# GpSimd's products given a choice of VectorE, and a scheduler that counts their shared port, in a hybrid LRU, GLA and SSD mixer

## The chip, the core and the metric

The kernel runs on one core of one Trainium2 chip. The metric is the device time in microseconds from launch to end on that core; shorter is better. The core's engines run side by side and wait for each other by semaphores. In the rows below PE is TensorE (PEld its weight loads), DVE is VectorE, ACT is ScalarE, POOL is GpSimd, SP the queue that issues the DMAs. Each engine works through its own queue strictly in the order in which the program lists it, so an instruction that waits holds up all that stand behind it.

## The reference, cut to what matters

Two layers (DEPTH = 2) work on 512 latent tokens and 256 context tokens of width 1024, all in float32. Layer 1 computes no output for the context tokens.

```python
s = h @ w_in                                    # one input projection feeds three branches
ya = bidir(lru_scan,    gates(conv(s[0])))      # h_t = a_t h_{t-1} + sqrt(1 - a_t^2) (i_t x_t)
yb = bidir(gla_chunked, q, k, v, logg)          # gated linear attention
yc = bidir(ssd_chunked, x*dt, dt*A, B, C)       # Mamba-2 state-space duality, in chunks
    # per chunk: m = cb * exp(cum_t - cum_s);  y = m x + (C state) exp(cum)
    #            state = state * exp(cum_end) + B^T (x * decay)
pa = (ya * silu(s[1])) @ w_pa
pb = (rmsnorm(yb) * silu(s[5])) @ w_pb
pc = rmsnorm((yc + d*x) * silu(s[7])) @ w_pc
out = x + gate * rmsnorm((g0*pa + g1*pb + g2*pc) @ w_out)
```

## The kernel before

**Tiling.** Every activation lies with 128 channels on the partitions and the tokens (768 in layer 0, the last 512 of them in layer 1) along the free axis. Each weight tile of 1024 columns comes by DMA (`raw`), is split into a high part (`wh`, a cast, by ACT or DVE) and the rest (`wl = raw - wh`, a subtraction on DVE), and the projections are three matmuls each (high by high, high by low, low by high) into the PSUM tiles `pp`. `ahead` counts the halves split in advance. Other matmuls and transposes write the PSUM tiles `aux`.

**Stages.** A layer runs through the SSD branch (32 heads in four groups `g`, each in two half groups `hg` of four heads), then GLA, then LRU, then the output projections. While a branch's small operations run, PE does the projections of the next items, `pc` and the gates, whose order is a fixed list.

**The SSD stage.** For each half group three streams run side by side. `ssd_states` goes over the chunks in both directions: `ssd_update` forms `xw` (the inputs scaled by their decay), the next state `sb` or `sf` as the old one scaled by `etr`, the split of `xw` into `xwh` (cast) and `xwl` (subtraction), three matmuls, and the sum into the new state. `ssd_ms` forms the 128x512 matrix `rr`: a DMA brings it, ACT adds a bias per head, DVE merges the two directions (`pred`, a COPY_PREDICATED), ACT takes the exponential, and then it is multiplied by `cb`. `ssd_scan` forms `y`, tokens on the partitions: `xt` times `kd`, plus matmul results, each scaled by `tokp` into `yi` and added. `y` is then transposed and multiplied into `gz`. `ssd_finish` adds four squares (`r`) and norms.

**The LRU stage.** `lru_rec` forms, for each of eight blocks and two directions, `w` as the square of `av` (128x768), and then `w`, `th`, `hf` and `hb` on DVE by products and scans.

**What goes where.** Helpers record one operation each: `tt` (product or sum of two tensors), `sub`, `copy`, `stt`, `ts`, `act`, `mm`. In `tt`, the argument `pool=True` sends the operation to POOL without a choice. So it stands with `xw`, the state products `sb` and `sf`, the product `rr` by `cb`, `y` from `xt` and `kd`, the sums of squares `r` and the square of `av`. `sub` with `pool=True`, `copy` and `affine` already let the scheduler choose between two engines.

**The scheduler.** The order in every queue is made when the program is built. Each stream is a generator that yields its next operation. `Sched.loop` takes, again and again, the operation that could start first by a model of the engines (`start_of`: when the engine is free and the data there, plus 200 ns for a hop between engines and a slack for the engine), with priorities for ties. Where an operation has several ways, it takes the one whose modelled start plus cost is least. The costs are straight lines:

```python
    def gcost(self, n):
        return 2.4 * n + 100
...
    def vcost(self, n, x, fast=False):
        return (0.52 if fast and x.space != PSUM else 1.04) * n + 69
```

No stretch of one engine by another is in this model.

## Time and profile before

| | us |
|---|---|
| median of 3 runs | 2781.73 (2781.67 to 2783.38) |
| the profiled execution | 2780.03 |
| its span, from the first instruction to the last | 2778.3 |
| mean granted clock of PE | 0.992 |

The profiled execution is longer than its span by 1.7 us, which lie around the instructions. Its rows tell, by engine and stage, how long instructions ran, and in which order. An instruction's row begins when it is taken up and ends when it is done. The next one of the same engine may be taken up before that, so the distance from one start to the next is what an instruction costs a full queue, and its duration is what an instruction that waits for it sees. The ends of matmuls are modelled, so PE's idle time shows best as that of its weight loads, PEld. By the source lines, the stages stand in the span so: the SSD stage of layer 0 from about 105 to 690, its LRU stage from about 1150 to 1400, the SSD stage of layer 1 from about 1640 to 2110, its LRU stage from about 2500 to 2660.

### The profile page before, as it was taken

To read this page: it belongs to the slowest core of one execution; us is meant where nothing else is said; L and a number is where in the kernel's file an instruction comes from. 1 tells how busy PE (TensorE), PEld (TensorE's weight loads), DVE (VectorE), ACT (ScalarE), POOL (GpSimd) and SP (SyncE) were. 2 spreads that over 40 slices of the span, in tenths; PEclk is the share of its full clock that TensorE was granted. 3 is DMA by queue.
4 is the path that set the end of the run, shared out by engine and by line. 5 is a ranking of instruction groups with operands and counts; after the bars stand their busy time and mean duration, and the time that the engine had idled before them with its cause. 6 is when DMAs were issued, how large, how long until landed. Compare 5 with 4: busy or idle time off the path is not lost.

```text
span 2778.3 us, 42828 instructions
## 1 busy us (share of the span) xinstructions
PE 2701.1 (97%) x16166; PEld 2344.8 (84%) x16166; DVE 2099.5 (76%) x3920; ACT 1186.7 (43%) x2274; POOL 584.2 (21%) x684
## 2 busy tenths in 40 slices
PE   7999999999999999999999999999999999999998
PEld 5888888888888888888889878788888888888877
DVE  5688988888555554668956879989897866568987
ACT  5355545454413331226622554545453333245732
POOL 1143525334000000001100224445251000001100
PEclk9999999999999999999999999999999999999999
DMA  6242323333352223552256434333334532243255
GB/s 212 73 126 69 113 68 102 79 96 93 102 182 73 73 61 94 158 162 57 76 169 209 140 89 109 84 91 105 86 107 114 167 84 76 81 147 103 54 158 195
DMA packets 448255, 307.99 MB, mean 111 GB/s; under 512 B 17189, under 2 KB 423281, under 8 KB 448049
## 3 DMA queue, kind: packets, MB, share of 16 engines
q1 hardware_dynamic: 448048, 305.26, 38.1%
q8 instruction: 127, 2.08, 0.3%
q14 instruction: 80, 0.65, 0.1%
HBM read 273.15 MB, written 32.06 MB: 110 GB/s over the span
## 4 chain that ended last, share of the span: by engine, by line
PE 74%; DVE 18%; issue 3%; DMA 2%; ACT 2%; POOL 1%; SPq 0%; DVEq 0%; POOLq 0%; ACTq 0%
PE pp L394 61%; PE aux L394 10%; DVE wl L343 2%; PE aux L398 2%; DVE r L364 2%; DVE xa L364 1%; DVE wh L329 1%; DMA ada<-in_ada_w_dram 1%; DVE xwl L343 1%; DVE rr L388 1%; DMA rr<-cumd 1%; PE aux L530 1%; DVE y L360 1%; DVE hf L360 0%; DVE xwh L329 0%
## 5 line engine op out<-in xcount | busy, mean ns | idle before, releaser
L394 PE MATMUL pp<-hl,wh 128*128 128x256 f32 (+2 forms) x2624 | 768.8, 354 | 0.2 <-DVE hl L343 0.2
L394 PE MATMUL pp<-hh,wh 128*128 128x256 f32 (+2 forms) x2624 | 761.5, 353 | 7.6 <-DVE xa L364 5.6
L394 PE MATMUL pp<-hh,wl 128*128 128x256 f32 (+2 forms) x2624 | 761.6, 352 | 0.6 <-DVE wl L343 0.6
L394 PEld LDWEIGHTS pp<-hh,wh 128*128 128x128 f32 (+1 forms) x2624 | 487.2, 189 | 68.6 <-ACT av L319 3.9
L394 PEld LDWEIGHTS pp<-hl,wh 128*128 128x128 f32 (+1 forms) x2624 | 489.0, 189 | 62.1 <-issue 2.6
L394 PEld LDWEIGHTS pp<-hh,wl 128*128 128x128 f32 (+1 forms) x2624 | 488.2, 189 | 61.1 <-DVE wl L343 1.0
L343 DVE TENSOR_TENSOR wl<-raw,wh 128x512 fp32r<-128x512 f32 (+1 forms) x628 | 467.8, 748 | 44.6 <-ACT wh L328 15.3
L329 DVE CAST wh<-raw 128x512 fp32r<-128x512 f32 (+1 forms) x401 | 191.7, 478 | 369.1 <-PE pp L394 362.8
L319 ACT ACTIVATE rr<-rr,tokp 128x128 f32<-128x128 f32 x640 | 202.5, 390 | 108.6 <-DMA rr<-cumd 108.2
L328 ACT CAST wh<-raw 128x512 fp32r<-128x512 f32 (+1 forms) x227 | 138.7, 617 | 241.3 <-PE pp L394 203.5
L319 ACT ACTIVATE r<-pp 128x768 f32<-128x768 f32 (+1 forms) x112 | 78.6, 702 | 253.1 <-PE pp L394 250.9
L360 POOL TENSOR_TENSOR xw<-xt,tokp 128x256 f32<-128x256 f32 x160 | 121.8, 761 | 270.0 <-ACT xt L328 188.6
L712 POOL TENSOR_SCALAR ss<-ss 128x1 f32<-128x1 f32 x52 | 14.2, 272 | 698.1 <-ACT ob L319 665.6
L360 POOL TENSOR_TENSOR w<-av 128x768 f32<-128x768 f32 x32 | 53.3, 1665 | 422.3 <-ACT av L319 355.5
L360 POOL TENSOR_TENSOR rr<-rr,cb 128x512 f32<-128x512 f32 x80 | 110.7, 1383 | 123.1 <-ACT rr L319 118.2
L394 PE MATMUL pp<-oh,wh 128*128 128x512 f32 (+1 forms) x384 | 121.1, 365 | 0.0
L394 PE MATMUL pp<-ol,wh 128*128 128x512 f32 (+1 forms) x384 | 120.8, 365 | 0.0
L394 PE MATMUL pp<-oh,wl 128*128 128x512 f32 (+1 forms) x384 | 119.4, 361 | 0.0
L394 PE MATMUL pp<-yh,wh 128*128 128x512 f32 (+1 forms) x384 | 116.9, 358 | 1.3 <-DVE r L364 1.3
L394 PE MATMUL pp<-yh,wl 128*128 128x512 f32 (+1 forms) x384 | 116.9, 358 | 0.0
L394 PE MATMUL pp<-yl,wh 128*128 128x512 f32 (+1 forms) x384 | 115.7, 355 | 0.0
L394 PE MATMUL pp<-wh,hl 128*128 128x256 f32 x384 | 108.9, 284 | 0.0
(270 smaller groups left out, 5343.4 us busy)
## 6 DMA issues: line engine op xcount, KB each, us to landing
raw<-in_w_in_dram SPq DMA_DIRECT2D x208, 512.0 KB
rr<-cumd SPq DMA_DIRECT2D x160, 256.0 KB
raw<-in_w_out_dram SPq DMA_DIRECT2D x40, 512.0 KB
raw<-in_w_pc_dram SPq DMA_DIRECT2D x32, 512.0 KB
raw<-in_ada_w_dram SPq DMA_DIRECT2D x32, 512.0 KB
ada<-in_ada_w_dram SPq DMA_DIRECT2D x8, 1024.0 KB
raw<-in_w_pb_dram SPq DMA_DIRECT2D x16, 512.0 KB
raw<-in_w_pa_dram SPq DMA_DIRECT2D x16, 512.0 KB
```

The costliest lines, as they stand in the source:

```text
L319: self.nc.scalar.activation(out, in_, func, **kw)
L328: yield from self.any_op([("ACT", self.acost(n, in_), lambda: self.nc.scalar.copy(out, in_)), ("DVE", self.vcost(n, in_, True), lambda: se ...
L329: ("DVE", self.vcost(n, in_, True), lambda: self.nc.vector.tensor_copy(out, in_))],
L343: ways = [("DVE", self.vcost(n, a), lambda: self.nc.vector.tensor_tensor(out, a, b, ALU.subtract))]
L360: yield from self.op("POOL" if pool else "DVE", [out], [a, b], cost, lambda: eng.tensor_tensor(out, a, b, op))
L364: lambda: self.nc.vector.scalar_tensor_tensor(out, a, s, b, op0, op1))
L388: lambda: self.nc.vector.copy_predicated(out, mask, data))
L394: lambda: self.nc.tensor.matmul(out, lhsT, rhs, start=start, stop=stop))
L398: yield from self.op("PE", [out], [in_, idn], 108, lambda: self.nc.tensor.transpose(out, in_, idn))
L530: yield from self.op("PE", [ps], [self.scf, w], w.free_size() / 2.4, lambda: self.nc.tensor.matmul(out, lt, w, start=k < 4, stop=k >= 4, t ...
L712: yield from self.op("POOL", [r], [ss], 150, lambda: self.nc.gpsimd.tensor_scalar(r, ss, 1.0 / width, EPS, ALU.mult, ALU.add))
```

## The change

Four things are edited. `tt` with `pool=True` now has two ways, DVE first and POOL second, and the scheduler takes the one with the earlier modelled end. The scheduler keeps, for DVE and for POOL, the last six modelled spans in which it used the port that both share: every POOL operation, and every DVE operation marked with `port` whose tensors are all outside PSUM. `shared` lengthens an operation's modelled cost by the time in which it overlaps such spans of the other engine, both where a choice is made and where the operation is entered. The marks are set in `any_op` (by default), `stt`, `ts` and `vcopy`. Nothing that is computed changes.

```diff
--- before.py
+++ after.py
@@ -151,6 +151,7 @@
         self.cells = {}
         self.eng_free = {"PE": 0.0, "DVE": 0.0, "ACT": 0.0, "POOL": 0.0, "SP": 0.0}
         self.dma_free = 0.0
+        self.port = {"DVE": [], "POOL": []}
         self.warm_up = HAM_WINDOW
         self.act_set = None
         self.seq = 0
@@ -184,14 +185,21 @@
                 r = c.r + slack
         return r
 
-    def op(self, eng, outs, ins, cost, emit):
-        yield from self.any_op([(eng, cost, emit)], outs, ins)
-
-    def any_op(self, ways, outs, ins):
-
+    def op(self, eng, outs, ins, cost, emit, port=False):
+        yield from self.any_op([(eng, cost, emit)], outs, ins, port)
+
+    def shared(self, eng, start, cost):
+
+        for a, b in self.port["POOL" if eng == "DVE" else "DVE"]:
+            cost += max(0.0, min(b, start + cost) - max(a, start))
+        return cost
+
+    def any_op(self, ways, outs, ins, port=True):
+
+        port = port and all(x.space != PSUM for x in outs + ins if x is not None and not isinstance(x, (int, float)))
         outs = [self.cell(o) for o in outs]
         ins = [self.cell(i) for i in ins if i is not None and not isinstance(i, (int, float))]
-        yield ("op", ways, outs, ins)
+        yield ("op", ways, outs, ins, port)
         eng, cost, emit = ways[self.way]
         start = self.start_of(eng, outs, ins)
         if eng == "PE":
@@ -203,6 +211,9 @@
         extra = emit()
         if isinstance(extra, int):
             cost += extra
+        if eng == "POOL" or (eng == "DVE" and port):
+            cost = self.shared(eng, start, cost)
+            self.port[eng] = self.port[eng][-5:] + [(start, start + cost)]
         if eng == "SP":
             self.eng_free[eng] = start + 470
             self.dma_free = max(start, self.dma_free) + cost
@@ -255,6 +266,8 @@
                 if c[0] == "op":
                     for w, (eng, cost, _) in enumerate(c[1]):
                         t = self.start_of(eng, c[2], c[3], LAT + SLACK[eng])
+                        if len(c[1]) > 1 and (eng == "POOL" or (eng == "DVE" and c[4])):
+                            cost = self.shared(eng, t, cost)
                         if w == 0 or t + cost < t0 + c0:
                             t0, c0, w0 = t, cost, w
                     k = (t0, 0 if s.urgent and s.urgent() else s.prio, s.seq)
@@ -355,13 +368,16 @@
         return (0.52 if fast and x.space != PSUM else 1.04) * n + 69
 
     def tt(self, out, a, b, op, pool=False):
-        eng = self.nc.gpsimd if pool else self.nc.vector
-        cost = self.gcost(out.free_size()) if pool else self.vcost(out.free_size(), a)
-        yield from self.op("POOL" if pool else "DVE", [out], [a, b], cost, lambda: eng.tensor_tensor(out, a, b, op))
+
+        n = out.free_size()
+        ways = [("DVE", self.vcost(n, a), lambda: self.nc.vector.tensor_tensor(out, a, b, op))]
+        if pool:
+            ways.append(("POOL", self.gcost(n), lambda: self.nc.gpsimd.tensor_tensor(out, a, b, op)))
+        yield from self.any_op(ways, [out], [a, b])
 
     def stt(self, out, a, s, b, op0, op1):
         yield from self.op("DVE", [out], [a, s, b], self.vcost(out.free_size(), a) + 60 * (not isinstance(s, float)),
-                           lambda: self.nc.vector.scalar_tensor_tensor(out, a, s, b, op0, op1))
+                           lambda: self.nc.vector.scalar_tensor_tensor(out, a, s, b, op0, op1), True)
 
     def ts(self, out, a, s1, s2, op0, op1=None, pool=False):
         eng = self.nc.gpsimd if pool else self.nc.vector
@@ -373,11 +389,11 @@
                 eng.tensor_scalar(out, a, s1, s2, op0)
             else:
                 eng.tensor_scalar(out, a, s1, s2, op0, op1)
-        yield from self.op("POOL" if pool else "DVE", [out], [a, s1, s2], cost, emit)
+        yield from self.op("POOL" if pool else "DVE", [out], [a, s1, s2], cost, emit, True)
 
     def vcopy(self, out, in_):
         yield from self.op("DVE", [out], [in_], self.vcost(out.free_size(), in_, True),
-                           lambda: self.nc.vector.tensor_copy(out, in_))
+                           lambda: self.nc.vector.tensor_copy(out, in_), True)
 
     def scan(self, out, a, b, init):
         yield from self.op("DVE", [out], [a, b, init], self.vcost(out.free_size(), a),
```

In the program that comes out, POOL has 433 instructions for 689, DVE 4109 for 3922 and ACT 2251 for 2184; PE and SP have as many as before. By kind, counted in the two programs:

| operation | POOL before | POOL now |
|---|---|---|
| `rr` by `cb`, 128x512 | 80 | 5 |
| states `sb` and `sf` by `etr`, 128x256 | 128 | 10 |
| square of `av`, 128x768 | 32 | 3 |
| sums of squares `r`, 128x512 and 128x768 | 24 | 6 |
| `y` from `xt` and `kd`, 128x256 | 80 | 72 |
| `xw`, 128x256 | 160 | 154 |

What left POOL stands on DVE. Of the operations that had a choice already, 34 casts `wh` and 26 casts `xwh` have gone from DVE to ACT. In the SSD stage of layer 1 alone, 30 of 32 `rr`, 61 of 64 state products, 9 of 12 sums `r`, 5 `xw` and 4 `y` have gone to DVE, and 12 casts `wh` and 12 `xwh` from there to ACT; in that of layer 0, 45 of 48 `rr`, 57 of 64 state products, 9 of 12 sums `r`, 1 `xw` and 4 `y`, and 16 `wh` and 14 `xwh`.

Queue of POOL in the SSD stage of layer 1, third half group, before (a name's number is that of the buffer):

```order
L360 TENSOR_TENSOR xw_18384<-xt_17995,tokp_16548 128x256
L360 TENSOR_TENSOR sb_18386<-sb_18306,etr_16549 128x256
L360 TENSOR_TENSOR rr_18335<-rr_18335,cb_18264 128x512
L360 TENSOR_TENSOR xw_18436<-xt_17995,tokp_16548 128x256
L360 TENSOR_TENSOR sb_18438<-sb_18386,etr_16549 128x256
L360 TENSOR_TENSOR xw_18505<-xt_17995,tokp_16548 128x256
L360 TENSOR_TENSOR sb_18507<-sb_18438,etr_16549 128x256
```

The same place of POOL's queue now:

```order
L375 TENSOR_TENSOR xw_18380<-xt_17975,tokp_16548 128x256
L375 TENSOR_TENSOR xw_18494<-xt_17975,tokp_16548 128x256
L375 TENSOR_TENSOR xw_18534<-xt_17975,tokp_16548 128x256
L375 TENSOR_TENSOR xw_18574<-xt_17975,tokp_16548 128x256
L375 TENSOR_TENSOR xw_18615<-xt_17975,tokp_16548 128x256
L375 TENSOR_TENSOR xw_18668<-xt_17975,tokp_16548 128x256
L375 TENSOR_TENSOR y_18681<-xt_17975,kd_18310 128x256
```

The products `rr` and `sb` that stood between two `xw` are gone; only `xw` and `y` are left.

Queue of DVE at that place, before, from the merge of an `rr`:

```order
L388 COPY_PREDICATED rr_18335<-mlt,rr_18338 128x512
L329 CAST xwh_18394<-xw_18384 128x256
L343 TENSOR_TENSOR xwl_18395<-xw_18384,xwh_18394 128x256
L364 SCALAR_TENSOR_TENSOR r_18321<-r_18378,r_18321 128x768
L343 TENSOR_TENSOR wl_18381<-raw_18214,wh_18380 128x512
L364 SCALAR_TENSOR_TENSOR gz_17748<-gz_17748,p_222_791,r_18049 128x512
L360 TENSOR_TENSOR sb_18386<-sb_18386,aux_18402 128x256
```

And now:

```order
L404 COPY_PREDICATED rr_18326<-mlt,rr_18329 128x512
L373 TENSOR_TENSOR sb_18319<-sb_18319,aux_18352 128x256
L373 TENSOR_TENSOR sb_18382<-sb_18319,etr_16549 128x256
L380 SCALAR_TENSOR_TENSOR r_18308<-r_18369,r_18308 128x768
L356 TENSOR_TENSOR xwl_18387<-xw_18380,xwh_18386 128x256
L373 TENSOR_TENSOR rr_18326<-rr_18326,cb_18268 128x512
L356 TENSOR_TENSOR wl_18306<-raw_18149,wh_18305 128x512
L380 SCALAR_TENSOR_TENSOR gz_17662<-gz_17662,p_222_802,r_18092 128x512
L356 TENSOR_TENSOR wl_18419<-raw_18199,wh_18418 128x512
L373 TENSOR_TENSOR sb_18382<-sb_18382,aux_18401 128x256
L373 TENSOR_TENSOR xw_18448<-xt_17975,tokp_16548 128x256
L373 TENSOR_TENSOR sb_18452<-sb_18382,etr_16549 128x256
```

Two products `sb` by `etr`, the product `rr` by `cb` and one `xw` now stand among the splits `xwl` and `wl`; four other instructions lie between the merge of `rr` and its product.

Queue of DVE in the LRU stage of layer 0, before, at the first `w` of a block:

```order
L329 CAST wh_13313<-raw_13147 128x512
L343 TENSOR_TENSOR wl_13314<-raw_13147,wh_13313 128x512
L364 SCALAR_TENSOR_TENSOR w_2462_13309<-w_2462_13309,th_13192 128x768
L364 SCALAR_TENSOR_TENSOR th_13250<-th_13250,xa_13141 128x768
L343 TENSOR_TENSOR wl_13346<-raw_13147,wh_13345 128x512
```

And now:

```order
L342 CAST wh_13310<-raw_13150 128x512
L356 TENSOR_TENSOR wl_13311<-raw_13150,wh_13310 128x512
L373 TENSOR_TENSOR w_2464_13313<-av_13314 128x768
L380 SCALAR_TENSOR_TENSOR w_2464_13313<-w_2464_13313,th_13213 128x768
L380 SCALAR_TENSOR_TENSOR th_13254<-th_13254,xa_13143 128x768
L373 TENSOR_TENSOR w_2464_13313<-av_13342 128x768
L380 SCALAR_TENSOR_TENSOR w_2464_13313<-w_2464_13313,th_13274 128x768
```

The two squares of `av`, which POOL made before, stand in DVE's queue, each right ahead of the instruction that reads it.

## Rows read from the trace of the kernel before

**Rows 1.** The page: busy time of each engine, and the chain that ended last

```profile
PE 2701.1 (97%) x16166; PEld 2344.8 (84%) x16166; DVE 2099.5 (76%) x3920; ACT 1186.7 (43%) x2274; POOL 584.2 (21%) x684
...
PE 74%; DVE 18%; issue 3%; DMA 2%; ACT 2%; POOL 1%; SPq 0%; DVEq 0%; POOLq 0%; ACTq 0%
```

**Rows 2.** Busy us (instructions): span, PE, PEld, DVE, ACT, POOL; PEclk, DMA, GB/s

```profile
105.00:690.00 585.00, 580.02 (x3547) 511.70 (x3546) 502.88 (x950) 292.55 (x669) 241.71 (x264) 1.00 0.34 92
1640.00:2110.00 470.00, 457.66 (x2496) 384.79 (x2495) 427.85 (x813) 238.05 (x538) 211.48 (x237) 1.00 0.36 96
1255.00:1400.00 145.00, 140.49 (x835) 123.75 (x835) 132.69 (x174) 97.86 (x127) 20.30 (x12) 1.00 0.26 69
```

**Rows 3.** Waits of PEld, 1600 to 2120: us in total, times, longest

```profile
PEld aux L394 <- DVE xwl L343: 10.1, 21, 1.2
PEld aux L394 <- DVE xwh L329: 5.9, 10, 1.0
...
PEld aux L398 <- POOL rr L360: 2.6, 3, 1.0
```

**Rows 4.** The same waits, 100 to 700

```profile
PEld aux L394 <- DVE xwl L343: 3.3, 10, 1.0
...
PEld aux L394 <- DVE xwh L329: 1.9, 3, 0.8
```

**Rows 5.** Timeline, all engines: start us, us, instruction, [idle before <-releaser]

```profile
1815.87 0.63 ACT L319 ACTIVATE rr<-rr 128x512 f32<-128x512 f32 x1 [0.34 <-DVE rr L388]
...
1816.58 1.38 POOL L360 TENSOR_TENSOR rr<-rr,cb 128x512 f32<-128x512 f32 x1 [0.32 <-ACT rr L319]
...
1816.73 1.50 DVE L343 TENSOR_TENSOR xwl<-xw,xwh 128x256 fp32r<-128x256 f32 x1
...
1818.29 0.19 PEld L394 LDWEIGHTS aux<-xwl,btok 128*128 128x128 f32 x1 [1.18 <-DVE xwl L343]
1818.29 0.38 PE L394 MATMUL aux<-xwl,btok 128*128 128x256 f32 x1 [0.74 <-DVE xwl L343]
```

**Rows 6.** Timeline of DVE in the LRU stage of layer 0

```profile
1322.23 0.95 DVE L364 SCALAR_TENSOR_TENSOR th<-th,xa 128x768 f32<-128x768 f32 x1
1323.10 0.68 DVE L343 TENSOR_TENSOR wl<-raw,wh 128x512 fp32r<-128x512 f32 x1
1323.70 0.42 DVE L329 CAST wh<-raw 128x512 fp32r<-128x512 f32 x1
```

**Rows 7.** Timeline of DVE in the SSD stage of layer 1

```profile
1693.91 0.41 DVE L343 TENSOR_TENSOR xwl<-xw,xwh 128x256 fp32r<-128x256 f32 x1
1694.24 0.41 DVE L360 TENSOR_TENSOR y<-y,aux 128x256 f32<-128x256 f32 x1
```

**Rows 8.** Groups of POOL, 1640 to 2110: xcount | busy us, mean ns | idle

```profile
L360 POOL TENSOR_TENSOR xw<-xt,tokp 128x256 f32<-128x256 f32 x79 | 61.4, 778 | 84.3 <-DVE xwl L343 41.1 <-ACT xt L328 35.3 <-DVE xt L329 7.2
L360 POOL TENSOR_TENSOR rr<-rr,cb 128x512 f32<-128x512 f32 x32 | 44.5, 1390 | 33.5 <-ACT rr L319 32.9 <-DMA rr<-cumd 0.3
L360 POOL TENSOR_TENSOR sb<-sb,etr 128x256 f32<-128x256 f32 x32 | 26.4, 825 | 34.9 <-DVE sb L360 28.1 <-ACT sb L328 4.5 <-DVE sb L329 2.3
L360 POOL TENSOR_TENSOR sf<-sf,etr 128x256 f32<-128x256 f32 x32 | 25.2, 786 | 40.9 <-DVE sf L360 28.9 <-DVE sf L329 5.1 <-ACT sf L328 3.8
```

**Rows 9.** Groups of DVE, 1640 to 2110

```profile
L343 DVE TENSOR_TENSOR wl<-raw,wh 128x512 fp32r<-128x512 f32 x105 | 89.7, 854 | 4.0
L360 DVE TENSOR_TENSOR y<-y,yi 128x256 f32<-128x256 f32 x64 | 39.0, 609 | 1.8
L343 DVE TENSOR_TENSOR xwl<-xw,xwh 128x256 fp32r<-128x256 f32 x62 | 37.7, 608 | 1.0
L329 DVE CAST wh<-raw 128x512 fp32r<-128x512 f32 x56 | 33.6, 601 | 8.4 <-PE pp L394 8.3
```

**Rows 10.** Groups of DVE, 1255 to 1400

```profile
L364 DVE SCALAR_TENSOR_TENSOR th<-th,xa 128x768 f32<-128x768 f32 x12 | 13.9, 1162 | 0.0
...
L360 DVE TENSOR_TENSOR hf<-hf,g 128x768 f32<-128x768 f32 x6 | 9.5, 1587 | 0.0
```


## Prediction

> **What bounds the kernel now.** I read the page first. PE is busy 2701.1 of 2778.3 us, and the chain that ended last runs 74% of the span over PE and 18% over DVE [rows 1]. So time is PE's, and another engine counts only where PE waits for it. The table by stage says where that can be: POOL works almost only in the two SSD stages (241.7 of 585 us, 211.5 of 470) and is nearly idle elsewhere, and DVE is fullest in the same places: 502.9 of 585, 427.9 of 470, and 132.7 of 145 in the LRU stage of layer 0 [rows 2]. DVE thus has 82, 42 and 12 us left there.
>
> The third view is what PE's weight loads wait for. In the SSD stage of layer 1 they wait 10.1 us for `xwl`, 5.9 for `xwh` and 2.6 for POOL's `rr` [rows 3]; in that of layer 0, 3.3 and 1.9 us for the first two [rows 4]. That is 23.8 us, all that this change can reach directly in PE's queue; the rest of the two stages is matmuls back to back.
>
> The fourth view is one such wait in full [rows 5]. POOL starts a product `rr` at 1816.58 and needs 1.38 us. DVE takes up an `xwl` at 1816.73 and holds it for 1.50 us, to 1818.23, although the same shape takes 0.41 in a quiet place [rows 7]: it ended after POOL did. PE's load for it then starts at 1818.29, after 1.18 us idle, and its matmul after 0.74. The `xwl` was late by 1.09 us, which is the whole of that wait. Averages say the same: in that stage `wl` takes 854 ns against 0.68 us where POOL is quiet, `y` and `xwl` 609 and 608 against 0.41, the cast `wh` 601 against 0.42 [rows 9, 6, 7]. Over 105, 64, 62 and 56 instructions that is 18.3 + 12.7 + 12.3 + 10.1 = 53 us of DVE's time spent held up beside POOL, in one stage.
>
> **The change, part by part.**
>
> Added to DVE. What one more product costs a full queue is the distance of starts: 0.87 us for 768 columns, 0.60 for 512 [rows 6], 0.33 for 256 [rows 7]. SSD stage of layer 1: 30 `rr` x 0.60 + 61 states x 0.33 + 9 sums x 0.60 + 9 `xw` and `y` x 0.33 = 18.0 + 20.1 + 5.4 + 3.0 = 46.5 us. Off it go 12 casts `wh` x 0.42 = 5.0; the casts `xwh` have no quiet row here and I leave them uncounted (between nothing and 5). Added: 41.5 us. SSD stage of layer 0: 45 x 0.60 + 57 x 0.33 + 9 x 0.87 + 5 x 0.33 - 16 x 0.42 = 48.6 us, which fits into its 82 us even if nothing else changed. LRU stage of layer 0, in the 145 us shown: 12 squares x 0.87 = 10.4 us; layer 1 moves 13 of 16 and not all.
>
> Taken from DVE: the holding up. In layer 1's stage POOL loses 30 x 1.390 + 31 x 0.825 + 30 x 0.786 = 91 of its 211.5 us by three kinds alone [rows 8, 2], 43%. If DVE is held in proportion to POOL's time, 43% of 53 = 23 us come back. What stays held is what `xw` and `y` hold. A bound below is nothing (the splits that remain collide with `xw` as often as before), one above is all 53. I take 23, which the POOL rows give. Row and rule: the Trainium skill, "SBUF — State Buffer", "Who interferes with whom", says that a VectorE instruction with two SBUF inputs and a GpSimd instruction that reads SBUF exclude each other for the whole instruction. The `xwl` above agrees: it was not slowed but ended after the other. By that rule a long holder costs by the square of its length, and of the four kinds in the POOL rows the three that go have 65% of the squares against 58% of the time, so that the relief would be 26 us in place of 23.
>
> Layer 1's SSD stage: 41.5 - 23 = +18 us on DVE, 446 of 470. LRU of layer 0: `th` and `hf` give back 12 x (1.162 - 0.95) + 6 x (1.587 - 0.95) = 6.3 us [rows 10, 6], so +4 in 12 us left. I charge the SSD stages nothing, since DVE's idle time there covers it; if that cover is gone it costs the 18 us. The LRU stages have the thinnest cover; I charge half of 4 us, and about as much in layer 1: +3 in all.
>
> Taken from PE: its waits. Each of the 21 waits for `xwl` is 0.48 us long on average [rows 3], and an `xwl` is late by 0.20 for itself on average, more by the `xw` and `xwh` that it waits for. `rr` is the longest holder and nearly leaves POOL, and the order is now made by a model that knows of the holding up, so PE's queue should have the matmul on `xwl` further back, behind projections that are ready. Between nothing and all of 23.8 us I take two thirds, nearer to all because of the one wait shown whole: -16 us.
>
> Queues. On POOL, `xw` stood behind `rr` and `sb`, and waits of POOL for the exponential (32.9 us) and for `sb` (28.1) stood ahead of it [rows 8]; now only `xw` and `y` are left, so `xw` comes earlier. It gains PE nothing by itself while `xwl` frees the one `xw` buffer late. On DVE, a product `rr` now waits in the queue for the exponential, which takes 0.63 us [rows 5], with `xwl`, `wl` and the next state behind it. Two to six other instructions lie between the merge and the product in nearly all cases, at 0.33 to 0.87 us each, and that covers it; uncovered, each product would hold DVE for up to 0.63 us, 19 us over the 30 of layer 1. SP's queue has the same 797 instructions; `rr` buffers come free a little sooner. ACT's extra casts lie in the half of its time that it is idle (238 of 470 busy).
>
> Sum: -16 + 3 = -13 us. The profiled execution took 2780.0 us, so 2767; the median of the runs shown is 1.7 us above it, so 2769.
>
> **The rivals.**
>
> *No change.* The waits for `xwl` are replaced by others of the same size: DVE is 18 us fuller, and what was late for the port is late for the queue. For it: PE has little to gain. Against it: the wait shown whole ends with the port. Time 2782, give or take 5. The Trainium skill, "Perfetto Trace Analysis", "Optimizing Scalar/DVE Operations", notes that moving work between these two engines might not help because they share a port; the rows bear out the sharing, not yet the conclusion.
>
> *Slower: DVE becomes what bounds layer 1's SSD stage.* The change sends work from an engine with 211 of 470 us busy to one with 428. The point from which it decides is the 42 us of idle time. If the holding up does not fall (41.5) and the products `rr` wait for the exponential (19), DVE is short by 18 us there, and the LRU stages, without relief, lose the rest up to 7: 2782 + 18 + 7 = 2807. With half the relief it is 2792 to 2797.
>
> *More than forecast.* All 23.8 us of waits go and the LRU stages cost nothing, since the square that `w` waits for now comes sooner: 2782 - 28 = 2754 with a few more waits for sums behind the same port.
>
> That the change might not do what it says is excluded by the two programs: POOL lists 433 instructions for 689.
>
> **How the numbers follow.** The forecast, 8 to 20 us faster: 0.45. More than that: 0.11. No change: 0.22. Slower: 0.22. A measurement of this kernel can tell about 0.2%, 5.6 us. So faster by more than that 0.56, within it 0.22, slower 0.22. The range leaves out the upper half of the slower case and little below the larger gain: 2752 to 2796. For the forecast alone it is 2762 to 2774.
>
> **What the profile would show.** Right: `xwl`, `y` and `wl` in layer 1's SSD stage nearer to 500, 500 and 770 ns; PEld's waits for `xwl` and `xwh` there at a third of 16 us; DVE busy some 440 to 450 of a stage that is about 460 long; the LRU stages within 2 us. Wrong: DVE's mean durations as before, which breaks the relief; new waits of DVE for ACT's `rr`, of PE for `y`, sums or `wl`; a stage of layer 1 longer than 470 with DVE full.

## The result, and the profile after

The changed kernel takes 2746.9 us (median of 4 runs, 2745.1 to 2749.6) against 2781.7 us before: ratio 0.988, 95% interval 0.986 to 0.989. Its profiled execution took 2748.7 us, its span is 2747.0 us against 2778.3, so 31.3 us shorter. It was forecast to get 13 us faster, with a range down to 2752 us: the sign was right and the size too small by more than half.

The page of the changed kernel, its line of busy time (answers to [rows 1]):

```profile
PE 2681.9 (98%) x16166; PEld 2341.2 (85%) x16166; DVE 2097.2 (76%) x4107; ACT 1214.9 (44%) x2341; POOL 302.3 (11%) x428
```

DVE has 187 instructions more and 2 us less of busy time; POOL's time has halved. PE has the same 16,166 matmuls in its row and is busy 19.2 us less, but its weight loads only 3.6 us less. The ends of matmuls are modelled, so a part of each wait stands as busy time in PE's own row: in [rows 5] the weight loads idle 1.18 us for one `xwl` and PE 0.74. By the weight loads, 27.7 of the 31.3 us that the kernel gained were idle time of PE. Their waits of more than 0.15 us, added up over the whole program, were 137.6 us and are 111.2. At the lower of the two levels of its granted clock (1.2 GHz; the other is 2.4) PE stood 46.9 us before and 38.8 now.

The table by stage, columns as in [rows 2]: first the same two stretches, then the SSD stages of both layers cut to their new length, then the LRU stage of layer 0.

```profile
105.00:690.00 585.00, 579.45 (x3565) 516.23 (x3564) 510.88 (x1038) 310.82 (x705) 118.65 (x148) 0.99 0.34 92
1640.00:2110.00 470.00, 466.97 (x2542) 396.13 (x2541) 434.15 (x910) 251.71 (x566) 107.81 (x131) 1.00 0.38 101
...
105.00:686.00 581.00, 575.45 (x3542) 512.66 (x3541) 509.74 (x1036) 308.84 (x702) 118.65 (x148) 0.99 0.34 93
1633.00:2088.00 455.00, 451.97 (x2491) 384.22 (x2490) 425.51 (x894) 245.90 (x560) 108.42 (x131) 1.00 0.38 100
1250.00:1398.00 148.00, 141.99 (x836) 125.04 (x835) 135.88 (x185) 98.02 (x129) 0.00 (x0) 0.99 0.24 65
```

The SSD stage of layer 1 is some 14 us shorter, and DVE, with 41.5 us of work more by the forecast's count, is busy 425.5 us there against 427.9. The waits of PE's weight loads in that stage, 1600 to 2100 us (answers to [rows 3]):

```profile
PEld aux L410 <- DVE xwl L356: 4.7, 12, 1.9
...
PEld aux L410 <- DVE xwh L342: 1.1, 4, 0.3
```

Together 5.8 us for 16.0 before, and none is left for POOL's `rr`. DVE's groups in 1640 to 2110 us (answers to [rows 9]):

```profile
L356 DVE TENSOR_TENSOR wl<-raw,wh 128x512 fp32r<-128x512 f32 x111 | 83.1, 750 | 4.6 <-ACT wh L341 0.6 <-DVE wh L342 0.5
L373 DVE TENSOR_TENSOR y<-y,yi 128x256 f32<-128x256 f32 x64 | 30.2, 472 | 1.8
...
L356 DVE TENSOR_TENSOR xwl<-xw,xwh 128x256 fp32r<-128x256 f32 x59 | 24.8, 421 | 0.6
...
L373 DVE TENSOR_TENSOR rr<-rr,cb 128x512 f32<-128x512 f32 x30 | 22.6, 754 | 0.0
```

and POOL's first three there (answers to [rows 8]):

```profile
L375 POOL TENSOR_TENSOR xw<-xt,tokp 128x256 f32<-128x256 f32 x73 | 61.7, 845 | 216.5 <-DVE xwl L356 150.2 <-ACT xt L341 61.5 <-PE aux L410 2.1
L375 POOL TENSOR_TENSOR y<-xt,kd 128x256 f32<-128x256 f32 x28 | 20.5, 732 | 40.1 <-PE aux L414 33.4 <-DVE kd L373 3.7 <-DVE wl L356 2.9
L358 POOL TENSOR_TENSOR xwl<-xw,xwh 128x256 fp32r<-128x256 f32 x20 | 16.7, 836 | 33.9 <-ACT xwh L341 33.9
```

DVE is held up less than forecast: `wl` 750 ns (forecast 770), `y` 472 (500), `xwl` 421 (500). Most of what the forecast said the profile would show is there, and the time is still 22 us below it. What is not there: DVE at 440 to 450 us (it is 425.5), and the LRU stage of layer 0 within 2 us (the next table). One wait is new and of the kind that was to speak against the forecast, 3.1 us of PE for a `y` in layer 0's SSD stage.

**Where the time went.** Both traces hold 12,288 matmuls on `pp`. If the start of the k-th of them in one is subtracted from that in the other, at nine values of k, this is what each stretch gained (minus) or lost, in us; the stretches are named by times of the kernel before:

| stretch before | what runs | after |
|---|---|---|
| 0 to 691 | start, SSD of layer 0 | -5.2 |
| 691 to 1288 | GLA of layer 0 | -0.2 |
| 1288 to 1436 | LRU of layer 0 | +2.9 |
| 1436 to 1648 | outputs of layer 0, start of layer 1 | -5.0 |
| 1648 to 2117 | SSD of layer 1 | -13.9 |
| 2117 to 2482 | GLA of layer 1 | -2.6 |
| 2482 to 2668 | LRU of layer 1 | -1.7 |
| 2668 to 2768 | outputs of layer 1 | -6.3 |

These add up to -32.0. They are of one execution each, and 19 executions of the kernel before took from 2773.2 to 2782.4 us in one series, so a stretch by itself tells no more than some us. The two SSD stages have 19 of it, and 14 us lie in four stretches between and behind them in which POOL hardly works. Part of these 14 has a source of its own. In the stretch from 1436, PE stood 6.8 us at 1.2 GHz for 13.7 before, which is worth up to 3.4 of its 5.0 us. In the last stretch DVE, with the split of a weight behind it in its queue, stood idle 5.01 us for a DMA before, and the same sum goes without that wait now:

```profile
2686.19 0.69 DVE L360 TENSOR_TENSOR r<-r,r 128x512 f32<-128x512 f32 x1 [5.01 <-DMA r<-me]
...
2652.36 0.69 DVE L373 TENSOR_TENSOR r<-r,r 128x512 f32<-128x512 f32 x1
```

Three of the runs below have such a wait of 5.1 to 5.4 us there (the old order moved, counting alone, the squares), and their last stretch gains 0.9 us or loses 1.2 and 0.9. Whether the order or the single execution decides on it is not shown. No relief of a port shared with POOL explains these 14 us, so the experiments ask for the cause itself: is it the work that moved, or the order that a planner writes when it counts the port?

### The profile page after: what moved, and what is told of

It is laid out like the page before. It is cut to its first block, busy times and chain, and to the rows that moved or that the text cites. A ratio compares the mean times of both kernels' runs of the same rounds, so it can differ in the third digit from the quotient of the medians.

```text
span 2747.0 us, 42626 instructions
## 1 busy us (share of the span) xinstructions
PE 2681.9 (98%) x16166; PEld 2341.2 (85%) x16166; DVE 2097.2 (76%) x4107; ACT 1214.9 (44%) x2341; POOL 302.3 (11%) x428
## 5 line engine op out<-in xcount | busy, mean ns | idle before, releaser
L356 DVE TENSOR_TENSOR wl<-raw,wh 128x512 fp32r<-128x512 f32 (+1 forms) x628 | 442.1, 707 | 48.4 <-ACT wh L341 15.1
L342 DVE CAST wh<-raw 128x512 fp32r<-128x512 f32 (+1 forms) x367 | 161.3, 439 | 336.7 <-PE pp L410 321.2
L341 ACT CAST wh<-raw 128x512 fp32r<-128x512 f32 (+1 forms) x261 | 160.1, 617 | 243.2 <-PE pp L410 202.7
L410 PE MATMUL pp<-wl,hh 128*128 128x256 f32 x384 | 108.8, 283 | 0.0
L410 PE MATMUL pp<-wh,hh 128*128 128x256 f32 x384 | 108.7, 283 | 0.0
L332 ACT ACT_TABLE_LOAD x75 | 96.2, 1283 | 17.2 <-PE pp L410 11.8
```

The costliest lines, as they stand in the source:

```text
L332: self.nc.scalar.activation(out, in_, func, **kw)
L341: yield from self.any_op([("ACT", self.acost(n, in_), lambda: self.nc.scalar.copy(out, in_)), ("DVE", self.vcost(n, in_, True), lambda: se ...
L342: ("DVE", self.vcost(n, in_, True), lambda: self.nc.vector.tensor_copy(out, in_))],
L356: ways = [("DVE", self.vcost(n, a), lambda: self.nc.vector.tensor_tensor(out, a, b, ALU.subtract))]
L410: lambda: self.nc.tensor.matmul(out, lhsT, rhs, start=start, stop=stop))
```

## The experiments

Medians of one series are compared by their ratio to the kernel before on the same chip. Each kernel's queues are written anew by the scheduler unless the text says otherwise.

**Moving without a new order, and the new order without moving.** Theory A is the forecast's. First: the scheduler of before, which plans `rr`, the states, the sums and the squares as POOL's, but they are issued to DVE, each at its planned place.

```diff
-        eng = self.nc.gpsimd if pool else self.nc.vector
+        eng = self.nc.gpsimd if pool and not to_dve else self.nc.vector
         cost = self.gcost(out.free_size()) if pool else self.vcost(out.free_size(), a)
```

> The planner of the kernel before, its costs and its order, with the products rr, the states, the sums and the squares issued to VectorE at the place at which the old plan had put them on GpSimd; xw, y and the rest stay on GpSimd. Theory A (the gain is VectorE's relief: long holders of the port leave): the moved work alone makes the gain, 2750 to 2760 us, with wl, y and xwl in layer 1's SSD stage under 790, 520 and 470 ns. Theory B (the gain is the new order made by a planner that counts the port): without the planner it is 2775 to 2800 us, VectorE fuller and no better placed. Theory C (the matrices and states come sooner, 0.6 us in place of 1.4): as A in time, but the means of wl, y and xwl stay where they were.

Measured: 2776.3 us, ratio 1.000 (0.999 to 1.001). DVE's groups in 1640 to 2110 us of this run:

```profile
L343 DVE TENSOR_TENSOR wl<-raw,wh 128x512 fp32r<-128x512 f32 x105 | 77.6, 739 | 4.2 <-PE pp L394 0.5
...
L360 DVE TENSOR_TENSOR y<-y,yi 128x256 f32<-128x256 f32 x64 | 28.4, 443 | 1.5
L343 DVE TENSOR_TENSOR xwl<-xw,xwh 128x256 fp32r<-128x256 f32 x62 | 27.3, 440 | 1.0
```

The three are as short as in the changed kernel (739, 443 and 440 ns for 750, 472 and 421), and nothing is gained. Theory A falls, and C with it: `rr` and the states are on DVE here as there. DVE as a whole has no less to do, 433.5 us of these 470 for 427.9 before because the moved products take what the others give back:

```profile
1640.00:2110.00 470.00, 459.66 (x2503) 386.19 (x2502) 433.50 (x921) 240.53 (x538) 98.75 (x129) 1.00 0.36 97
```

(Nor does the old plan hold the moved work in its clock of DVE; the runs below turn on that clock.) The Trainium skill, "Perfetto Trace Analysis", "Optimization Strategies", advises to optimize the engines for which TensorE waits; here `wl` became 13% and `y` and `xwl` 27 and 28% shorter just where PE waits for them, and the time stayed, but with more of them in the queue it is no test of shorter instructions alone.

Second: the order of the changed kernel, with the same products issued to POOL at their places (the way to DVE keeps its cost, and only its engine is POOL's).

> The order and the plan of the changed kernel, with the products rr, the states, the sums and the squares sent back to GpSimd at their places in it. Theory A: VectorE is held up again, 2780 to 2800 us, as before or worse because the plan thinks of them as short. Theory B: the order carries the gain, 2750 to 2765 us.

Measured: 2775.2 us, ratio 0.999 (0.998 to 1.000). So theory B in its plain form falls as well: neither the move without its order nor the order without its move gives anything. In this order the move is worth 1.1%, in the old one nothing. Both runs have a plan that is wrong about the chip: the first leaves the moved work out of DVE's clock, the second holds products for short ones of DVE's that run on POOL.

**Half of the change each.** Counting alone: every product goes to POOL as before, the planner counts the port.

```diff
         if pool:
+            ways = ways[1:]
```

(after POOL's way has been added). Choice alone: `shared` returns the cost unchanged.

> The planner counts the shared port, but every product has to go to GpSimd as before (only splits and casts may still choose). Theory A: 2775 to 2785 us, since the holders are all there. Theory B: 2750 to 2765 us.

Measured: 2740.3 us, ratio 0.986 (0.985 to 0.988), more than theory B's range allowed: the whole gain, with nothing moved but splits and casts. DVE's groups in 1640 to 2110 us of this run are as long as in [rows 9]:

```profile
L356 DVE TENSOR_TENSOR wl<-raw,wh 128x512 fp32r<-128x512 f32 x112 | 92.9, 831 | 12.8 <-ACT wh L341 9.4 <-PE pp L411 0.8
L356 DVE TENSOR_TENSOR xwl<-xw,xwh 128x256 fp32r<-128x256 f32 x71 | 42.3, 596 | 1.7 <-ACT xwh L341 1.1
L373 DVE TENSOR_TENSOR y<-y,yi 128x256 f32<-128x256 f32 x64 | 37.3, 582 | 1.9
```

What has changed is seen in a timeline of this run, at an `xwl` that runs into POOL's `rr` as the one in [rows 5] does:

```profile
1823.37 1.55 POOL L375 TENSOR_TENSOR rr<-rr,cb 128x512 f32<-128x512 f32 x1
...
1823.70 1.51 DVE L356 TENSOR_TENSOR xwl<-xw,xwh 128x256 fp32r<-128x256 f32 x1
...
1825.21 0.51 PE L411 MATMUL pp<-hl,wh 128*128 128x256 f32 x2
...
1825.91 0.19 PEld L411 LDWEIGHTS aux<-xwl,btok 128*128 128x128 f32 x1
...
1826.02 0.28 PE L411 MATMUL aux<-xwl,btok 128*128 128x256 f32 x1
```

The split takes 1.51 us beside a product of 1.55, just as before, and ends at 1825.21. But its weights are loaded only at 1825.91: matmuls of projections stand ahead of it, and nothing waits. On the sharing itself, the Trainium skill, "SBUF — State Buffer", "Who interferes with whom", says that two such instructions exclude each other whole; both kernels' rows agree (1.50 us beside 1.38, 1.51 beside 1.55). It says what the split costs and not whether PE pays it: that is the order's doing.

> Products may choose their engine, but the planner does not count the port: 16 rr, 27 states, 8 sums and 3 squares stay on GpSimd, and 76 splits xwl go there in place of 33. Theory A: most of the gain, 2752 to 2765 us; what is lacking is what the splits and the products that stay hold up. Theory B: little of it, 2772 to 2785 us.

Measured: 2758.8 us, ratio 0.993 (0.992 to 0.995): about half of the gain, between the two theories. The moved work is now in the planner's clock of DVE, which runs later for it.

**Clock or choice.** The count enters the scheduler at two places: into the clocks (when an engine is free) and into the choice between engines. Each alone, all products on POOL:

```diff
-                        if len(c[1]) > 1 and (eng == "POOL" or (eng == "DVE" and c[4])):
-                            cost = self.shared(eng, t, cost)
```

> As the kernel that counts the port and leaves every product on GpSimd, but the count goes only into the planner's clocks (when an engine is free, when a result is there), not into the choice of an engine: 70 casts xwh and the splits stay where the kernel before has them or go to GpSimd. Theory H (the count makes the planner's clock of VectorE agree with the chip, and PE's order is written from that clock): 2738 to 2750 us. Theory K (the count works through the choices, casts to ACT and splits off GpSimd): 2768 to 2782 us.

Measured: 2739.6 us, ratio 0.986 (0.984 to 0.988).

> The reverse: the count goes only into the choice between engines, and the planner's clocks run on as if the port were not shared. Products on GpSimd. Theory H: 2765 to 2782 us, PE's order being as wrong as before. Theory K: 2738 to 2752 us.

Measured (the other place removed, `cost = self.shared(eng, start, cost)`): 2763.7 us, ratio 0.995 (0.993 to 0.996). The planner's clock gives all of the gain by itself, H; the choice of engines for splits and casts gives a good third of it when it stands alone, just below H's range and far from K's.

**A clock that knows nothing of the port.** The scheduler of before, no port counted, nothing given to another engine by hand; DVE's instructions are longer or shorter in its clock by one factor.

```diff
             cost += extra
+        if eng == "DVE":
+            cost *= 1.15
```

> The planner of the kernel before, no port counted, nothing moved, but each VectorE instruction is put down as 1.15 times as long in the planner's clock. Theory H: it corrects the mean lag (VectorE was held up 66 of 428 us in layer 1's SSD stage, 15%) but not the place of it: a part of the gain, 2748 to 2768 us. Theory P (the planner needs to know where the port is shared): 2772 to 2785 us.

Measured: 2735.3 us, ratio 0.984 (0.983 to 0.986), the lowest of the study though not clear of the next ones, and below H's range. No knowledge of the port is needed, and P falls.

> The planner of the kernel before with each VectorE instruction put down as 0.87 times as long in its clock: the same work on the same engines, planned too early instead of late. Theory L (what pays is the distance in PE's queue between a product of VectorE and the matmul that takes it, and a late clock makes it longer): slower than before, 2790 to 2815 us. Theory N (any new order shakes the waits out and comes out faster, whatever its sign): 2740 to 2775 us.

Measured with 0.87: 2819.6 us, ratio 1.015 (1.013 to 1.016), just above L's range. N falls: a new order is not better by being new. The waits of PE's weight loads in this run's SSD stage of layer 1 (1630 to 2160 us) have grown from those of [rows 3]:

```profile
PEld aux L396 <- DVE xwl L345: 14.9, 36, 2.0
PEld aux L396 <- DVE xwh L331: 6.0, 11, 0.9
```

> The kernel before with each VectorE instruction 1.30 times as long in the planner's clock (0.87 gave 2820, 1.15 gave 2735). Theory D with an upper end, as the factor together with the longer ranking showed: the plan thinks VectorE is full and holds back what is ready, 2745 to 2800 us. Without an upper end: 2700 to 2730 us.

Measured with 1.30: 2783.8 us, ratio 1.002 (1.001 to 1.003): the gain is gone. What DVE waits for in 100 to 710 us of this run:

```profile
DVE wh L331 <- PE pp L396: 43.0, 25, 3.5
DVE y L362 <- PE aux L396: 26.2, 29, 3.1
DVE sb L362 <- PE aux L396: 11.7, 13, 2.2
```

Here DVE stands idle for PE's results: the order puts the matmuls that it waits for too far back. Idle time of DVE costs nothing by itself, and PE's weight loads wait 125.3 us in this run, less than the 137.6 of before. What is lost is lost by PE's granted clock: it stood 73.0 us at 1.2 GHz for 46.9, and the mean is 0.984 to 0.987 in all ten executions, for 0.990 to 0.994 of the kernel before. What PE did ahead of such a fall is shown below, for all products on DVE.

**Distance by itself.** The same scheduler with its clocks untouched; a matmul is ranked as startable 2.0 us after its operands, not 1.2 (and the hop of 0.2 in both).

```diff
-SLACK = {"PE": 1200, "DVE": 100, "ACT": 100, "POOL": 0, "SP": 0}
+SLACK = {"PE": 2000, "DVE": 100, "ACT": 100, "POOL": 0, "SP": 0}
```

> The planner of the kernel before, clocks untouched, but a matmul is ranked as startable 2.0 us after its operand in place of 1.2 us, so that PE's order puts more projections ahead of it. Theory L: most of what the slower VectorE clock gave, 2738 to 2760 us. Theory H (only a clock that agrees with the chip helps, since the distance by itself was enough): 2772 to 2785 us.

Measured: 2749.7 us, ratio 0.990 (0.988 to 0.991): about as much as the change (the intervals overlap), by one number. It also answers a rival: that these runs gain because the scheduler hands casts from DVE to ACT. Here 7 `wh` and 5 `xwh` more are on ACT than before and DVE is busy 2095.0 us for 2099.5, and 1.0% is gained; the changed kernel's order with its products sent back has 34 and 26 more on ACT and gains nothing. With the factor 1.15 it is 57 `wh`, so a part of that run's further 0.6% may come from there. Together with the factor 1.15:

> The kernel before, nothing moved, no port counted, VectorE 1.15 times as long in the clock and matmuls ranked 2.0 us after their operands. Theory D: the distance is nearly enough with one of the two (2735 and 2750 us); both give little more or too much, 2728 to 2750 us. If distance had no upper end it would be 2710 to 2725 us.

Measured: 2750.2 us, ratio 0.990 (0.988 to 0.992). The two together give no more than the slack alone: it has an upper end, as D said.

**The worth of the move at equal clocks.** The choice alone with the factor 0.87 and with 1.15:

> Products may choose their engine, the port is not counted (2759 us so far), and the planner's clock for VectorE is shortened to 0.87 as in the run with the kernel before that came to 2820 us. Theory D (distance is all, relief of VectorE is worth nothing by itself): 2800 to 2825 us. Theory R (the products' move has a worth of its own, some 18 us at any distance): 2785 to 2800 us.

Measured: 2823.3 us, ratio 1.016 (1.014 to 1.017); with the products on POOL it was 1.015.

> As the run before, but the clock for VectorE lengthened to 1.15, as in the run with the kernel before that came to 2735 us. Theory D: 2732 to 2750 us, no better than with every product on GpSimd. Theory R: 2712 to 2730 us.

Measured: 2742.8 us, ratio 0.987 (0.985 to 0.988); with the products on POOL 0.984. Of the three factors, only at the plain costs does the choice give something (0.993 against 1). R falls.

> The changed kernel, choice and counting as they are, and each VectorE instruction 1.15 times as long in the planner's clock on top. Theory L: a further gain, 2725 to 2742 us against 2747. Theory H: the clock was right and is now late, 2745 to 2765 us.

Measured: 2741.1 us, ratio 0.987 (0.985 to 0.988), against 0.988 (0.986 to 0.989) for the change itself: the intervals overlap, and whether a further gain is there stays open.

**No sharing at all.** All products and splits on DVE alone, planned with plain costs and with the factor 1.15.

```diff
-        if pool:
+        if False:
```

> Every product and split may use VectorE alone: hardly anything holds the port, and the planner's clock is right without counting. 165 instructions are left on GpSimd. Theory H: as good as the changed kernel as long as VectorE is not full, 2742 to 2760 us. Theory F (VectorE gets too full, 60 us more work per SSD stage): 2765 to 2800 us.

Measured: 2775.5 us, ratio 0.999 (0.998 to 1.000): in F's range, not in H's. The table by stage for layer 1's SSD stage, and PE's longest waits there (1600 to 2120 us):

```profile
1640.00:2110.00 470.00, 453.65 (x2438) 387.00 (x2437) 440.93 (x1031) 233.58 (x516) 4.72 (x5) 0.96 0.35 94
```

```profile
PE aux L410 <- DVE xwh L342: 7.1, 5, 2.2
PE aux L410 <- DVE sf L373: 3.4, 4, 1.3
PE aux L414 <- DVE y L373: 3.3, 2, 1.9
```

POOL is gone from the stage, DVE has 29 us left in 470, and PE waits for casts, states and `y` that stand in DVE's queue: by the subtraction of the first section the stage loses 11.0 us. But these waits are not longer than those of before: in 1600 to 2120 us the waits of the weight loads add up to 27.0 us, for 32.8. The line of the stage says what is: a granted clock of PE of 0.96 for 1.00, that is, 34 us at 1.2 GHz for 3. Most of it is one place:

```profile
1776.00:1784.00 8.00, 4.43 (x22) 2.93 (x20) 7.90 (x21) 3.88 (x10) 0.00 (x0) 1.00 0.64 158
...
1791.00:1811.00 20.00, 13.84 (x46) 11.09 (x47) 17.52 (x49) 9.27 (x27) 0.73 (x1) 0.51 0.19 52
```

From 1776.6 to 1809.6 PE has no matmul on `pp`: its projections have run out, and it waits for `xwh`, `sf` and `y`. It was busy 4.43 us of the 8 ahead of the first fall of its clock. At 1.2 GHz a matmul of 512 columns on `pp` starts 0.43 us after the one ahead of it (at 1810), for 0.23 (at 1775). So 31 us more at that level cost up to 15 us, an estimate that covers the 11.0. All ten executions have a mean clock of 0.985 to 0.989. F's reason, a full DVE, is not what these rows show by themselves.

> All products and splits on VectorE (2775 us when planned with plain costs), now planned with each VectorE instruction 1.15 times as long. There is hardly a holder of the port, so the plain costs were right and these are too long. Theory L: 2735 to 2758 us, since the distance was what lacked. Theory H: no better, 2770 to 2785. Theory F (VectorE is simply too full): 2765 to 2790 us.

Measured: 2840.9 us, ratio 1.023 (1.021 to 1.025), above the ranges of all three theories. Its SSD stages by the same columns as [rows 2]:

```profile
100.00:730.00 630.00, 597.39 (x3558) 526.34 (x3557) 539.69 (x1164) 315.15 (x703) 15.01 (x18) 0.95 0.32 85
1660.00:2190.00 530.00, 489.82 (x2519) 414.67 (x2518) 465.61 (x1058) 247.29 (x540) 6.35 (x8) 0.93 0.33 88
```

DVE needs 540 and 466 us there. Times 1.15 that is 621 and 535 us, which is about what the stages last, 630 and 530, though PE idles 33 and 40 us in them and DVE 90 and 64. So the plan takes DVE for the bound and the order makes PE keep its pace. That is argued from these rows; no run isolates it. PE's granted clock has its part here too (0.95 and 0.93 in these lines): PE stood at 1.2 GHz 51 and 75 us longer than before, worth up to 26 and 38 of the 37 and 55 us that the two stages lose, by the estimate above.

**The squares.**

> The changed kernel with the 32 squares of av kept on GpSimd. In the LRU stage of layer 0 the changed kernel gives back 2.9 us, while runs with the squares on GpSimd gain 2 to 3 there. Theory S (the squares on VectorE cost that): the stage from 1288 to 1436 us gains, and the whole is 2738 to 2744 us. Theory E (it is the order of the rest): 2745 to 2752 us. If the squares' move is what shortens the last 100 us of layer 1 by 6 us, that goes lost: 2747 to 2752 us.

Measured (only `w2[:, d], av, av` is fixed on POOL): 2748.6 us, ratio 0.989 (0.987 to 0.991). By the same subtraction as above the LRU stage of layer 0 gains 1.8 us where the changed kernel loses 2.9, as S said of that stage (up to 1.7 us of the difference is PE's granted clock: 3.4 us at 1.2 GHz in the changed kernel, none here), and the last 100 us lose 0.9 where it gains 6.3. The whole is the same, above S's range; the execution whose stretches these are took 2753.3 us, 4.7 more than the median.

**A version by stages.** The count in the clock, and the factor 1.15 only where POOL has been idle for 5 us:

```diff
+        if eng == "DVE" and not any(start - q < 5000 for _, q in self.port["POOL"]):
+            cost *= 1.15
```

> Every product on GpSimd as in the kernel before. The planner's clock counts the port (the run that came to 2740 us), and where GpSimd has been idle for 5 us an instruction of VectorE is put down as 1.15 times as long. Theory D by stages (each stage keeps what it gained with its own lengthening: 12.0 and 14.8 us in the SSD stages from the count, 1.7, 3.3, 9.9, 4.6, 6.9 and 4.3 elsewhere from the factor): 2712 to 2728 us. If the gains of the stages do not add, 2733 to 2745 us.

Measured: 2737.8 us, ratio 0.985 (0.984 to 0.987). The gains of the stages don't add: the SSD stage of layer 1 gains 4.3 us in place of 14.8. PE's waits there are some 14 us shorter than before, but it stood 13.7 us at 1.2 GHz for 3.4.

**The distance in the traces.** Each of the 80 matmuls on an `xwl` in the SSD stage of layer 1 was paired, by its place in the program, with the split that it reads; its start less the end of that split is the reserve that the order left it on the chip. At 0.05 or 0.06 us the matmul had been waiting. Beside it stand the waits of PE's weight loads over the whole program and the time for which PE's clock stood at 1.2 GHz, of the same execution.

| kernel | median reserve, us | under 0.4 us, of 80 | PE's waits, us | at 1.2 GHz, us | ratio of time |
|---|---|---|---|---|---|
| clock x0.87 | 0.21 | 43 | 182.7 | 50.3 | 1.015 |
| old order, moved | 0.42 | 40 | 138.4 | 39.3 | 1.000 |
| before | 0.48 | 35 | 137.6 | 46.9 | 1 |
| choice, clock x0.87 | 0.57 | 32 | 183.5 | 50.5 | 1.016 |
| count in the choice | 0.65 | 34 | 126.3 | 29.2 | 0.995 |
| squares on POOL | 0.67 | 29 | 112.2 | 47.3 | 0.989 |
| choice only | 0.67 | 25 | 120.7 | 29.8 | 0.993 |
| after | 0.67 | 30 | 111.2 | 38.8 | 0.988 |
| new order, back | 0.70 | 25 | 138.7 | 41.0 | 0.999 |
| clock x1.15 | 0.77 | 24 | 101.8 | 17.2 | 0.984 |
| all on DVE | 0.85 | 20 | 121.6 | 75.5 | 0.999 |
| by stages | 1.23 | 14 | 93.7 | 52.0 | 0.985 |
| count only | 1.32 | 5 | 98.6 | 42.6 | 0.986 |
| count in the clock | 1.33 | 13 | 102.5 | 23.8 | 0.986 |
| choice, clock x1.15 | 1.43 | 13 | 94.5 | 51.8 | 0.987 |
| slack 2.0 us | 1.43 | 18 | 111.8 | 32.5 | 0.990 |
| clock x1.30 | 1.45 | 9 | 125.3 | 73.0 | 1.002 |
| all on DVE, x1.15 | 1.59 | 18 | 166.6 | 149.5 | 1.023 |
| after, clock x1.15 | 1.66 | 5 | 93.7 | 51.7 | 0.987 |
| x1.15 and slack 2.0 | 1.90 | 8 | 105.8 | 35.2 | 0.990 |

The shortest reserve goes with one of the longest times, and the reserves of more than 1 us with both the short times and two of the long ones. But it is one operand in one stage, and it doesn't order the rows: choice with x0.87 has more of it than before and is slower, and *after, clock x1.15* has nearly the most and is among the fastest. The order of the changed kernel with its products sent back has 0.70 us and no gain, because against the changed kernel it loses 26 us in five stretches, most of it elsewhere: 5.6, 4.8, 3.5, 3.6 and 8.4 us from the start to the end of layer 1's SSD stage.

The two columns beside it account for them. Half, because instructions at 1.2 GHz took about twice as long above: the change of PE's waits plus half the change of the time at 1.2 GHz gives the change of the span to within 6.2 us in all rows but *all on DVE, x1.15* (80 us by that sum, 60 measured). So the upper end is not the reserve alone: x1.30 and all on DVE have fewer waits than before and lose the gain by PE's granted clock; *all on DVE, x1.15* loses by both. This is a bookkeeping of the traces; no run sets the granted clock by itself.

## Why the prediction was wrong

- **PE bounds, and DVE counts where PE waits for it:** right.
- **Added to DVE, 41.5 us in layer 1's SSD stage, less 23 of relief:** the relief was mis-sized. DVE was forecast at 446 us there and is busy 425.5, 2.3 less than before, so by the forecast's count of the addition (the 12 casts `xwh` left out) some 44 us of the 53 came back, not 23. It hardly matters for the time: in the old order instructions as short, with the same products on DVE, gave nothing.
- **PE's waits, -16 us:** these rows went as forecast, from 16.0 to 5.8 us for `xwl` and `xwh` in layer 1, from 5.2 to 0.3 in layer 0 and to none for POOL's `rr`, together -17.7, and the two SSD stages gained 19 us. But the reason given first, that the port is relieved, is not needed for it, since counting alone keeps the port as busy (POOL 209.8 of 470 us in layer 1's stage for 211.5) and gains 14.6 us in layer 1's stage and 11.8 in layer 0's. The half sentence beside it was the cause: the order is made by a model that knows of the holding up, and PE's queue has the matmul further back.
- **23.8 us as "all that this change can reach directly in PE's queue": the step that failed.** It bounded the gain by five rows of waits in two stages, while a new order touches every wait of the program. PE's weight loads wait 137.6 us before and 111.2 after: beside the 17.7 us of the five rows, 8.7 us of other waits are gone, with no term in the sum. Up to 4 us more are PE's granted clock (8.1 us less at 1.2 GHz). Nor do the five rows bound the gain in their own stages: they are 5.2 us in layer 0's, which gained 11.8 under counting alone.
- **LRU stages, +3 us:** +2.9 in layer 0 and -1.7 in layer 1, so +1.2. The first goes with the squares, as forecast (with them on POOL it is -1.8), but for up to 1.7 us of PE's granted clock.
- **Queues:** the products `rr` stand behind the exponential without a wait of DVE (0.0 us of idle before 30 of them); right.
- **The rivals:** *no change* is what the move alone does, and what all products on DVE do. *Slower* is what came of the latter once it was planned at 1.15, with DVE as the bound of the plan and not of the chip, where it idled 90 and 64 us. *More than forecast* had the right size nearly, 2754, with the wrong mechanism.

The cause as the runs leave it: the order of before was written by a planner whose clock of DVE ran ahead of the chip, so PE's matmuls stood too close behind the splits and sums that they read. Its straight line gives an `xwl` 335 ns and a `wl` 601, which are the quiet distances of starts (0.33 and 0.60 us [rows 7, 6]); the 0.20 and 0.17 us by which their means in [rows 9] lie above the quiet durations are not in it. Three ways to plan more distance gain 1.0 to 1.6% without any move of the products: the count of the port in the clock, a factor of 1.15, a slack of 2.0 us; a factor of 0.87 loses 1.5%. The move itself is worth 1.1% in the order that the changed kernel has, 0.7% where only the choice is free, and nothing at the other two factors, so it depends on the order around it. Why each stretch gains as much as it does was not isolated; of the last 100 us the trace shows that a wait of DVE for a DMA went away.

## What to carry to other kernels

Where the order in every queue is written ahead from a cost model, a change of the model's costs is a change of every queue: price it over the whole program, and not by the waits beside the operations that it names. Before modelling a contention, scale one engine's cost in the planner up and down and look at the curve (here 0.87, 1, 1.15 and 1.30 gave 1.015, 1, 0.984 and 1.002), since one number may give what the model does. And the waits for the operands that a change names bound what these operands lost, not what an order can gain: add up all waits of the bounding engine first, and look at its granted clock beside them, since an order that lets its work run out pays there (here up to 15 us in one stage).

## What the runs showed of the hardware

Freed of POOL, DVE's instructions are a fifth to a third shorter: in the run with all products on DVE `wl` takes 685 ns in layer 1's SSD stage for 854, and `y` and `xwl` 423 for 609 and 608. That this was worth nothing to the time was not expected; the products that came over made up for it in DVE's busy time (433.5 and 440.9 us of the same 470 us for 427.9). The product `rr` takes 754 ns on DVE in the changed kernel and 683 in that run, for 1390 on POOL.
